# Which engine issues the stores of a DiT block kernel: from one queue to three

## The chip, the cores and the metric

The kernel runs on one core of one Trainium2 chip. The metric is the device time of one execution in microseconds (us); less is better. A core has five engines that run side by side, each through its own instruction stream in order: TensorE (PE, matmuls), VectorE (DVE), ScalarE (ACT), GpSimd (POOL) and SyncE (SP), which here issues DMAs and nothing else. A DMA moves data between HBM and the on-chip memory; it is issued by an instruction on one of these streams, and an instruction that has to wait for its data holds everything behind it in the same stream.

## The reference

One layer of a diffusion backbone, in float32: 2048 latent tokens of width 1024, and 256 context tokens that only supply the initial states of a scan.

```python
hx = modulate(rmsnorm(x, pre_norm_mix), mx[0], mx[1])
# token_mixers:
proj = h @ w_in
xbc = silu(dwconv(proj[..., OFF_XBC:OFF_DT], conv_w, conv_b))
y = y_f + y_b[:, ::-1] + d_skip[:, None] * xs      # a chunked scan in either direction
y = rmsnorm(y * silu(z), ssm_g)
p = pool_mixer(proj[..., OFF_POOL:], w_pool, pool_scale)   # box means on a 32x64 grid, minus the token
yx = concatenate([y, p]) @ w_out
x = x + mx[2] * rmsnorm(yx, post_norm_mix)
hx = modulate(rmsnorm(x, pre_norm_ffn), mx[3], mx[4])
# conv_ffn:
v, g = split(dwconv(hx @ w_up, conv_w, conv_b), 2)
x = x + mx[5] * rmsnorm((silu(g) * v) @ w_down, post_norm_ffn)
```

## The kernel before, in words

**Matmuls.** A float32 product is made of three passes: each operand is split into a high half (ScalarE, L120) and a low half (the rest, L123, on VectorE or GpSimd), and `mm3` (L151 to L153) multiplies high by high, high by low and low by high into the same PSUM bank. A low half is thus needed from the second pass (L152) on.

**Stages.** Times are those of the profiled execution.

- 0 to 560: the input projection in four blocks of 512 tokens, with the convolutions and the forward scan. Block 0 splits the weights (`wunit`, L130 to L139) and stores both halves to `wk_d`; blocks 1 to 3 load them back (L141). `pool_unit` writes `u_d` (L569) and `c_d` (L582); the scan writes `sb_d` (L535) and `y_d` (L544); the gate writes `sz_d` (L795).
- 556 to 680: `pool_mix`, eight steps (four groups, two halves): load a piece of `c_d` into a region of `XB` (L597) and one of `u_d` (L601), add shifted copies (L606), subtract (L615), multiply (L620), scale on ScalarE (L621), store `p_d` (L622). The region of `XB` is used again two steps later, and so L597 waits for the store of L622.
- 600 to 930: the backward scan, the product with `w_out`, the residual (`x1_d`, L837), the norm (`h_d`, L906) and sums of quarters (`hs_d`, L889).
- 975 to 1400: the up projection, upper half (p=1), as one level of a Strassen scheme with seven products per pair; 22 pairs. Four sums of weights per pair are split and kept in `wu_d` (L1072); the result goes to `act_d` (L1122).
- 1400 to 1837: the lower half (p=0), 11 steps of two pairs. The kept weights come back from `wu_d` (L1068). A step stores two tiles of `act_d` (L1124), and `act_sums` stores four sums to `s_d` (L1143); `down_sums` stores `ds_d` (L1152).
- 1837 to 2298: the down projection, again seven products. Its tiles `ar` come from `s_d` and `act_d` (L1203), its weights `rw` from `ds_d` or from the weight itself (L1191); both are split into `as` and `tc`. The rows of the result are stored to `out` (L1226).

**What sets the order.** The code is written as streams of work with priorities (`hot()`, `high_priority`). A scheduler with a simulated time line puts the instructions of each engine into an order before the program runs. On the chip each engine takes its list strictly in that order. Tiles live in small rings (six for `wo`, three for `ar`): an instruction that writes a tile waits until its former readers, a store among them, are done.

**Queues.** All loads and stores are issued by SyncE, about 1020 instructions in one list. A store there waits for the engine that makes its data, and the loads behind it wait with it. GpSimd (`G` in the code) makes small copies in the up stages: the two columns between the halves (L1104, L1105, L1107, L1108), one column of a sum (L1137) and of the last column (L1126). ScalarE is `S`, VectorE `V`.

## Time and profile before

| | us |
|---|---|
| median of 3 runs | 2299.97 (2297.82, 2299.97, 2303.13) |
| the profiled execution | 2301.18 |
| its span in the trace | 2298.1 |
| around the span | 3.1 |
| TensorE busy | 2117.2 (92%) |
| VectorE busy | 1639.7 (71%) |
| ScalarE busy | 902.8 (39%) |
| GpSimd busy | 452.1 (20%) |

A span is the time from the first to the last instruction in the trace. Busy shares are averages over stages that differ: a table by stage shows where TensorE stands still, and the list of its waits says what ended each stand-still. In the table by stage the columns after the busy times are the granted clock of TensorE as a share of full speed (PEclk; 1.00 is 2.4 GHz), the mean busy share of the DMA engines, and what they moved in GB/s. A timeline then gives the single instructions of one engine, with start and duration; the brackets behind a row hold the idle time before it and what ended it. "SPq" is SyncE's queue; a duration there is the time in which one DMA (or x2, two of them) was being issued, waits between the two included.

### The profile page before, as it was taken

Reading aid. Unit: us, or ns where it says so; the run is one execution under the profiler, and the core shown is the slowest. Engines: PE = TensorE matmul, PEld = TensorE weight load, DVE = VectorE, ACT = ScalarE, POOL = GpSimd, SP = SyncE. Lnnn points to the kernel's source line nnn. Section 1 sums busy time; section 2 is a strip of 40 time slices with the busy share of each in tenths; the row PEclk is TensorE's granted clock in tenths of the full one; section 3 lists DMA queues with packets and bytes.
Section 4 is the critical chain, followed back from the end, with each engine's and each line's share of the span. In section 5 each row is a group of like instructions: output and inputs, shape, how many; then the busy total and the mean of one; then the engine's idle time right before and its main releaser. Section 6 shows DMA issues by size and latency. Waiting matters only on the chain. (4 is left out here: it accounts for less than half of the span.)

```text
span 2298.1 us, 27242 instructions
## 1 busy us (share of the span) xinstructions
PE 2117.2 (92%) x9473; PEld 1684.1 (73%) x9473; DVE 1639.7 (71%) x2464; ACT 902.8 (39%) x1372; POOL 452.1 (20%) x553
## 2 busy tenths in 40 slices
PE   8798999899778788499999999999999969999998
PEld 4686777677456666388888887878888758888786
DVE  5777868977778567678878888878767654333666
ACT  4434433333324544445444445323333334333422
POOL 1533524525355443000001001000000000000000
PEclk9989999899899899799999999999999989999999
DMA  8856969869774658765566669999777585444364
GB/s 307 273 181 241 311 226 346 262 218 285 251 233 149 236 191 281 271 217 206 213 247 219 239 224 335 381 348 358 257 262 259 193 292 181 140 151 139 124 231 148
DMA packets 242970, 552.91 MB, mean 241 GB/s; under 512 B 52176, under 2 KB 101008, under 8 KB 238480
## 3 DMA queue, kind: packets, MB, share of 16 engines
q1 hardware_dynamic: 242832, 551.17, 68.2%
q8 instruction: 74, 1.21, 0.2%
q14 instruction: 64, 0.52, 0.1%
HBM read 369.56 MB, written 181.54 MB: 240 GB/s over the span
## 5 line engine op out<-in xcount | busy, mean ns | idle before, releaser
L152 PE MATMUL pu<-xcT,wo 128*128 128x512 f32 x704 | 278.7, 396 | 0.0
L151 PE MATMUL pu<-xcT,wo 128*128 128x512 f32 x704 | 278.6, 396 | 0.0
L153 PE MATMUL pu<-xcT,wo 128*128 128x512 f32 x704 | 276.9, 395 | 0.0
L151 PE MATMUL pu<-xcB,wo 128*128 128x512 f32 x528 | 210.1, 399 | 25.4 <-ACT wo L120 21.1
L151 PE MATMUL psf<-tc,as 128*128 128x512 f32 x528 | 204.5, 395 | 21.7 <-ACT tc L120 21.5
L123 DVE TENSOR_TENSOR as<-ar,as 128x1024 fp32r<-128x1024 f32 x66 | 80.8, 1224 | 193.6 <-ACT as L120 193.5
L152 PE MATMUL pu<-xcB,wo 128*128 128x512 f32 x528 | 210.0, 398 | 0.0
L153 PE MATMUL pu<-xcB,wo 128*128 128x512 f32 x528 | 208.4, 397 | 0.3 <-DVE wo L123 0.3
L152 PE MATMUL psf<-tc,as 128*128 128x512 f32 x528 | 206.0, 390 | 0.0
L151 PE MATMUL pu<-wh,hxh 128*128 128x512 f32 x384 | 156.2, 423 | 29.0 <-DVE eb L817 10.8
L153 PE MATMUL psf<-tc,as 128*128 128x512 f32 x528 | 179.7, 391 | 3.0 <-DVE as L123 3.0
L153 PE MATMUL pu<-hxh,wl 128*128 128x512 f32 (+2 forms) x448 | 165.1, 371 | 2.3 <-POOL wl L123 2.1
L123 POOL TENSOR_TENSOR wl<-wst,wh 128x1024 fp32r<-128x1024 f32 x48 | 122.6, 2554 | 225.9 <-ACT wh L120 202.3
L151 PE MATMUL pu<-hxh,wh 128*128 128x512 f32 (+2 forms) x448 | 164.9, 373 | 2.0 <-ACT wh L120 1.4
L152 PE MATMUL pu<-hxl,wh 128*128 128x512 f32 (+2 forms) x448 | 166.3, 372 | 0.0
L152 PE MATMUL pu<-wl,hxh 128*128 128x512 f32 x384 | 159.4, 415 | 5.3 <-POOL wl L123 5.3
L151 PEld LDWEIGHTS pu<-xcT,wo 128*128 128x128 f32 x704 | 132.9, 189 | 31.3 <-ACT wo L120 0.3
L152 PEld LDWEIGHTS pu<-xcT,wo 128*128 128x128 f32 x704 | 133.0, 189 | 31.1
L153 PEld LDWEIGHTS pu<-xcT,wo 128*128 128x128 f32 x704 | 132.5, 188 | 31.1
L153 PE MATMUL pu<-wh,hxl 128*128 128x512 f32 x384 | 153.9, 409 | 0.0
L120 ACT CAST as<-ar 128x1024 fp32r<-128x1024 f32 x66 | 69.5, 1054 | 214.5 <-PE psf L153 191.0
L120 ACT CAST wo<-rawu 128x512 fp32r<-128x512 f32 x132 | 81.6, 620 | 174.3 <-PE pu L153 168.6
(326 smaller groups left out, 4589.0 us busy)
## 6 DMA issues: line engine op xcount, KB each, us to landing
wu_d<-wo SPq DMA_DIRECT2D x88, 512.0 KB, 2.7
wo<-wu_d SPq DMA_DIRECT2D x88, 512.0 KB, 5.5
rawu<-in_w_up_dram SPq DMA_DIRECT2D x66, 512.0 KB, 4.0
wh<-wk_d SPq DMA_DIRECT2D x48, 512.0 KB, 6.7
wl<-wk_d SPq DMA_DIRECT2D x48, 512.0 KB, 5.8
ar<-s_d SPq DMA_DIRECT2D x44, 512.0 KB, 3.5
XB<-in_w_ada_b_dram SPq DMA_DIRECT2D x32, 512.0 KB, 6.3
wst<-in_w_out_dram SPq DMA_DIRECT2D x32, 512.0 KB, 4.7
```

The costliest lines, as they stand in the source:

```text
L120: S.copy(out=hi, in_=src)
L123: le.tensor_tensor(out=lo, in0=src, in1=hi.bitcast(F32), op=ALU.subtract)
L151: PE.matmul(o, lt[0], rt[0], start=start, stop=False, **kw)
L152: PE.matmul(o, lt[0], rt[1], start=False, stop=False, **kw)
L153: PE.matmul(o, lt[1], rt[0], start=False, stop=stop, **kw)
```

## The change

Every store but five instructions leaves SyncE. Stores of what ScalarE makes, and some others beside it, are issued by ScalarE (`S.dma_start`); the rest is issued by GpSimd (`G.dma_start`). On SyncE stay all loads, the two small stores of `gr_d`, and the last three rows of the output. In number, 108 DMAs go to ScalarE's stream, 104 of them in the first 930 us; about 270 go to GpSimd's. Nothing is computed in another way. The diff, without its lines of context:

```diff
@@ -134,9 +134,9 @@
-                for t, d_ in zip((hi, lo), kept):
+                for t, d_, e in zip((hi, lo), kept, (S, le)):
-                        nc.sync.dma_start(out=d_, in_=t.bitcast(F32))
+                        e.dma_start(out=d_, in_=t.bitcast(F32))
@@ -400,7 +400,7 @@
-            nc.sync.dma_start(out=rows_d, in_=csT)
+            S.dma_start(out=rows_d, in_=csT)
@@ -532,7 +532,7 @@
-            nc.sync.dma_start(out=sb_d[c * P:(c + 1) * P, :], in_=sb)
+            S.dma_start(out=sb_d[c * P:(c + 1) * P, :], in_=sb)
@@ -541,7 +541,7 @@
-            nc.sync.dma_start(out=y_d[c * P:(c + 1) * P, :], in_=y)
+            G.dma_start(out=y_d[c * P:(c + 1) * P, :], in_=y)
@@ -566,7 +566,7 @@
-        nc.sync.dma_start(out=u_d[g * P:(g + 1) * P, b * TB:(b + 1) * TB].rearrange("p (r c) -> p r c", c=GW),
+        S.dma_start(out=u_d[g * P:(g + 1) * P, b * TB:(b + 1) * TB].rearrange("p (r c) -> p r c", c=GW),
@@ -579,7 +579,7 @@
-        nc.sync.dma_start(out=c_d[g * P:(g + 1) * P, b * TB:(b + 1) * TB].rearrange("p (r c) -> p r c", c=GW),
+        G.dma_start(out=c_d[g * P:(g + 1) * P, b * TB:(b + 1) * TB].rearrange("p (r c) -> p r c", c=GW),
@@ -619,7 +619,7 @@
-        nc.sync.dma_start(out=p_d[g * P:(g + 1) * P, cols], in_=d)
+        S.dma_start(out=p_d[g * P:(g + 1) * P, cols], in_=d)
@@ -757,7 +757,7 @@
-                    nc.sync.dma_start(out=ct_d[:, :, b * TB:(b + 1) * TB], in_=CT)
+                    S.dma_start(out=ct_d[:, :, b * TB:(b + 1) * TB], in_=CT)
@@ -792,7 +792,7 @@
-            nc.sync.dma_start(out=sz_d[b * TB + i * P:b * TB + (i + 1) * P, :], in_=o)
+            S.dma_start(out=sz_d[b * TB + i * P:b * TB + (i + 1) * P, :], in_=o)
@@ -834,7 +834,7 @@
-                    nc.sync.dma_start(out=self.dst[t0:t0 + P, cs], in_=self.ys[i][:, cs])
+                    G.dma_start(out=self.dst[t0:t0 + P, cs], in_=self.ys[i][:, cs])
@@ -886,7 +886,7 @@
-        nc.sync.dma_start(out=hs_d[p][:, :, kk, :].rearrange("s p c -> p s c"), in_=hb)
+        G.dma_start(out=hs_d[p][:, :, kk, :].rearrange("s p c -> p s c"), in_=hb)
@@ -903,7 +903,7 @@
-            nc.sync.dma_start(out=h_d[b // 2][k, :, b % 2 * TB:(b % 2 + 1) * TB], in_=full[:, 0:TB])
+            S.dma_start(out=h_d[b // 2][k, :, b % 2 * TB:(b % 2 + 1) * TB], in_=full[:, 0:TB])
@@ -1037,7 +1037,7 @@
-        nc.sync.dma_start(out=h_d[0][:, :, i * P:(i + 1) * P].rearrange("k p t -> p k t"),
+        S.dma_start(out=h_d[0][:, :, i * P:(i + 1) * P].rearrange("k p t -> p k t"),
@@ -1069,7 +1069,7 @@
-                nc.sync.dma_start(out=wu_d[i][a - 1], in_=w.bitcast(F32))
+                G.dma_start(out=wu_d[i][a - 1], in_=w.bitcast(F32))
@@ -1119,9 +1119,9 @@
-            nc.sync.dma_start(out=dst[:, 1:2 * TB], in_=v[:, 0:2 * TB - 1])
+            G.dma_start(out=dst[:, 1:2 * TB], in_=v[:, 0:2 * TB - 1])
-            nc.sync.dma_start(out=dst, in_=v[:, 0:2 * TB])
+            G.dma_start(out=dst, in_=v[:, 0:2 * TB])
@@ -1140,7 +1140,7 @@
-            nc.sync.dma_start(out=s_d[q_][k], in_=o_)
+            G.dma_start(out=s_d[q_][k], in_=o_)
@@ -1149,7 +1149,7 @@
-        nc.sync.dma_start(out=ds_d[k], in_=t)
+        G.dma_start(out=ds_d[k], in_=t)
@@ -1172,7 +1172,7 @@
-    nc.sync.dma_start(out=act_d[1][1][:, :, 0].rearrange("k p -> p k"), in_=last)
+    G.dma_start(out=act_d[1][1][:, :, 0].rearrange("k p -> p k"), in_=last)
@@ -1223,7 +1223,7 @@
-            nc.sync.dma_start(out=out[t0:t0 + P, :], in_=y)
+            (nc.sync if th and j > 4 else G).dma_start(out=out[t0:t0 + P, :], in_=y)

```

**The entry to the down stage.** SyncE's list before, from the last load of kept weights of the up stage to the third tile of the down stage (`act_d_87` to `act_d_90` are the four parts of `act_d`; `s_d_91` to `s_d_94` the four sums; what stands behind a name is its number):

```order
L1068 DMA wo<-wu_d_3_185 128x1024
L1124 DMA act_d_87<-av 128x1024
L1124 DMA act_d_89<-av 128x1024
L1175 DMA act_d_90<-last 128x11x1
L1143 DMA s_d_91<-tt 128x1024
L1143 DMA s_d_93<-tt 128x1024
L1143 DMA s_d_92<-av 128x1024
L1143 DMA s_d_94<-av 128x1024
L1203 DMA ar<-s_d_92 128x1024
L1191 DMA rw<-ds_d 128x512
```

The same place of SyncE's list after the change:

```order
L1136 DMA tt<-act_d_88 128x1023
L1136 DMA tt<-act_d_90 128x1023
L1068 DMA wo<-wu_d_3_185 128x1024
L1203 DMA ar<-s_d_92 128x1024
L1191 DMA rw<-ds_d 128x512
```

The seven stores between the last `wo` and the first `ar` are gone from it. They now stand in GpSimd's list, between its copies:

```order
L1124 DMA act_d_87<-av 128x1024
L1137 COPY tt<-av 128x1
L1124 DMA act_d_89<-av 128x1024
L1126 COPY last<-av 128x1
L1137 COPY tt<-av 128x1
L1175 DMA act_d_90<-last 128x11x1
L1143 DMA s_d_91<-tt 128x1024
L1143 DMA s_d_93<-tt 128x1024
L1143 DMA s_d_92<-av 128x1024
L1143 DMA s_d_94<-av 128x1024
```

The store of `act_d_89` now comes before the two copies, which VectorE's first sum needs. On ScalarE and VectorE the order of this stretch is the same in both kernels.

**The pool mixer.** SyncE's list before, around the second and the third store of the upper groups:

```order
L544 DMA y_d<-y 128x512
L622 DMA p_d<-XB 128x1024
L601 DMA xr<-u_d 128x1024
L141 DMA wl<-wk_d_1_211 128x1024
L130 DMA wst<-in_w_out_dram 128x1024
L597 DMA XB<-c_d 128x1536
L622 DMA p_d<-XB 128x1024
```

ScalarE's list after the change, at this place (`DMAHW` is a counter of landed DMAs, eight of which SyncE and ScalarE share, so that a DMA waits for the one eight before it on its counter; for 55 of ScalarE's 108 DMAs that one is a load of SyncE):

```order
L621 ACTIVATE XB<-pb,pt 128x512 [waits PE_49]
L622 DMA p_d<-XB 128x1024 [waits DMAHW5_49,Activation_49]
L621 ACTIVATE XB<-pb,pt 128x512 [waits DMAHW3_49,PE_49]
L621 ACTIVATE XB<-pb,pt 128x512 [waits PE_49]
L508 ACT_TABLE_LOAD
```

The store follows the activation that makes its data, in the same list, and the activations behind it come after it.

**The upper half of the up stage.** GpSimd's list after the change, one pair (before, L1105 and L1104 took turns there and nothing else):

```order
L1072 DMA wu_d_1_115<-wo 128x1024
L1122 DMA act_d_88<-av 128x1023
L1072 DMA wu_d_0_114<-wo 128x1024
L1105 COPY sv<-un 128x2
L1072 DMA wu_d_2_116<-wo 128x1024
L1104 MEMSET un 128x2
L1105 COPY sv<-un 128x2
L1072 DMA wu_d_3_117<-wo 128x1024
L1104 MEMSET un 128x2
```

Five stores of 512 KB stand between the four small operations of a pair.

## Rows read from the trace of the kernel before

**Rows 1.** Stages: window, us, busy (count) of PE, PEld, DVE, ACT, POOL, then PEclk.
```profile
0.00:930.00 930.00, 819.68 (x3888) 632.46 (x3889) 693.11 (x1194) 365.88 (x611) 377.49 (x344) 0.94 0.73 250
...
975.00:1400.00 425.00, 425.00 (x1849) 344.06 (x1848) 358.06 (x507) 202.94 (x294) 35.56 (x85) 1.00 0.63 228
...
1837.00:1862.50 25.50, 4.03 (x12) 2.89 (x11) 15.52 (x14) 5.85 (x7) 0.31 (x2) 0.60 0.64 219
```

**Rows 2.** Waits of TensorE, whole span: us in total, times, longest.
```profile
PE psf L151 <- ACT tc L120: 21.5, 1, 21.5
PE pu L151 <- ACT wo L120: 21.1, 1, 21.1
...
PE pb L620 <- DVE XB L615: 9.4, 2, 8.0
...
PE pu L151 <- ACT wh L120: 8.7, 6, 2.4
```

**Rows 3.** Timelines of the engines, 1826 to 1863, by time: start, us, engine, line.
```profile
1826.24 19.26 SPq L1124 DMA_DIRECT2D act_d<-av  x2
...
1842.83 1.06 ACT L1117 ACTIVATE ag<-ag 128x1025 f32<-128x1025 f32 x1 [2.68 <-DVE ag L1113]
1843.92 1.23 DVE L1118 TENSOR_TENSOR av<-av,ag 128x1025 f32<-128x1025 f32 x1 [1.12 <-ACT ag L1117]
...
1849.33 1.22 DVE L1142 TENSOR_TENSOR av<-av 128x1024 f32<-128x1024 f32 x1
1849.33 1.58 SPq L1143 DMA_DIRECT2D s_d<-av  x2
1851.00 0.59 SPq L1203 DMA_DIRECT2D ar<-s_d  x1
...
1856.53 1.04 ACT L120 CAST as<-ar 128x1024 fp32r<-128x1024 f32 x1 [12.64 <-DMA ar<-s_d]
...
1858.26 0.62 ACT L120 CAST tc<-rw 128x512 fp32r<-128x512 f32 x1 [0.69 <-DMA rw<-ds_d]
...
1858.93 3.69 PE L151 MATMUL psf<-tc,as 128*128 128x512 f32 x8 [21.47 <-ACT tc L120]
...
1862.46 0.40 PE L152 MATMUL psf<-tc,as 128*128 128x512 f32 x1
```

**Rows 4.** Timelines of the engines, 570 to 612, by time, around the pool mixer.
```profile
579.38 3.52 SPq L544 DMA_DIRECT2D y_d<-y  x1
...
579.69 0.69 ACT L621 ACTIVATE XB<-pb,pt 128x512 f32<-128x512 f32 x1 [1.18 <-PE pb L620]
...
583.00 0.37 SPq L622 DMA_DIRECT2D p_d<-XB  x1
...
588.23 0.32 SPq L597 DMA_DIRECT2D XB<-c_d  x1
...
610.86 2.05 PE L620 MATMUL pb<-XB,junk 128*128 128x512 f32 x2 [8.02 <-DVE XB L615]
```

**Rows 5.** One source line, L906: count, ns min/median/max, first and last start.
```profile
L906 SPq DMA_DIRECT2D h_d<-t x24: 319/320/671, 784.5 to 919.7; - x24
```

**Rows 6.** Waits of SyncE's queue, whole span: us in total, times, longest.
```profile
SPq L139 <- ACT wh L120: 37.3, 12, 9.3
```

**Rows 7.** One of the costliest groups of the page: count, busy us, mean ns, idle before.
```profile
L123 POOL TENSOR_TENSOR wl<-wst,wh 128x1024 fp32r<-128x1024 f32 x48 | 122.6, 2554 | 225.9 <-ACT wh L120 202.3
```

**Rows 8.** GpSimd's groups by line in 975 to 1400, same columns.
```profile
L1105 POOL COPY sv<-un 128x2 f32<-128x2 f32 x43 | 31.3, 729 | 267.7 <-ACT un L1095 149.7 <-DVE un L1099 118.0
```

**Rows 9.** Timeline of VectorE 570 to 586: one form of L615 twice.
```profile
574.54 2.05 DVE L615 SCALAR_TENSOR_TENSOR XB<-XB,xr 128x1024 f32<-128x1024 f32 x1 [0.63 <-POOL XB L612]
...
582.73 1.22 DVE L615 SCALAR_TENSOR_TENSOR XB<-XB,xr 128x1024 f32<-128x1024 f32 x1
```

**Rows 10.** DMA issues on the page: count, KB each, us to landing.
```profile
wu_d<-wo SPq DMA_DIRECT2D x88, 512.0 KB, 2.7
...
act_d<-av SPq DMA_DIRECT2D x22, 512.0 KB, 5.2
```

## The prediction

> **What bounds the kernel now.** I read the table by stage first. In the up stage TensorE is busy without a gap, 425.00 of 425 us in its first half, at a granted clock of 1.00 [rows 1]. Nothing that a store does there can make it faster; it can only make it slower. The gaps lie elsewhere: the first 930 us, with TensorE busy 819.68 us, so 110 us short, and 25.5 us at the entry to the down stage, with 4.03 us of work [rows 1]. The list of TensorE's waits comes next. It has two waits of 21 us, one for `tc` at the entry to the down stage, one for `wo` at the entry to the up stage; the pool mixer stands at 9.4 us, the weights `wh` at 8.7 us [rows 2]. The first of these I follow in the timeline, since SyncE's queue is part of it; behind the second no store stands: the order of SyncE and ScalarE at the entry to the up stage is the same after the change but for the stores, and its chain runs over splits on VectorE. It is costed at nothing.
>
> **The entry to the down stage.** SyncE issues the two stores of `act_d` as one group from 1826.24 to 1845.50, because the second waits for the product on VectorE (L1118, 1843.92 and 1.23 long). The store of the last sum waits until 1850.5 for VectorE's last sum (L1142, from 1849.33). Only then, at 1851.00, comes the load of the first `ar`, although its data was stored long before. ScalarE gets it at 1856.53, `tc` follows at 1858.26, and TensorE begins at 1858.93 and comes to its second pass at 1862.46 [rows 3].
>
> After the change no store stands ahead of this load; it then waits for the end of a product of the up stage, by 1830, and both loads are there long before ScalarE is free. ScalarE is free at 1842.83 + 1.06 = 1843.9 [rows 3], and its list has the same order as before. So `as` ends at 1844.9, `tc` at 1845.6, and the eight matmuls of the first pass begin at 1845.6 instead of 1858.93. But the second pass needs low halves from VectorE, and there the four sums stand first, in both kernels. The copies on GpSimd that the first of them needs now come after the store of `act_d_89`. With x for the issue of a store on GpSimd, the sums begin at 1845.2 + x + 0.4. The fourth overwrites the tile that this store reads, so it waits for the landing; an `act_d` store landed 5.2 us after its issue in the middle [rows 10]. With x = 0.7 this is 1851.1, its end 1852.3, and two splits of 1.2 and 0.7 us (as the sum and the `tc` of this place) bring the second pass to 1854.2. That is 8.3 us earlier than 1862.46. TensorE has idled twice by then; if it goes once more through eight matmuls at 3.69 / 8 = 0.46 us instead of 0.23, 1.9 us are lost again, of which I take 1.3. **−7.0 us**, ends −9.5 (x = 0.3, a landing that isn't felt) and −3 (x = 3, a landing as late as 7 us).
>
> **The pool mixer.** Here a store on ScalarE follows its data at once. In the trace the activation L621 ended at 580.38, but the store went out at 583.00, behind one of `y_d` that held the queue for 3.52 us; the load that waits for its landing went out at 588.23, and TensorE's wait of 8.02 us at 610.86 stands at the end of what that load began [rows 4]. 583.00 − 580.38 = 2.6 us earlier: **−2.6 us**, ends −8 (the whole wait) and +4, since the stores of `c_d`, which the loads read, now come from GpSimd and may land later.
>
> **Loads out of the stores' shadow.** In the first 930 us SyncE waited for data of stores, with loads behind it: 37.3 us in twelve waits for `wh` alone [rows 6]. TensorE felt late weights with 8.7 us [rows 2]. I give a third of that back: **−3 us**, ends 0 and −15, the bound if most waits for weights and some of the chains behind them go.
>
> **ScalarE's new work.** 104 stores in the first 930 us. An issue took 0.32 us in the middle on SyncE [rows 5], so 33 us more on an engine that is busy 365.88 of 930 [rows 1]. No row shows an issue on ScalarE; I take SyncE's. Between none of it on the path and the busy share of 39% (13 us) I take a tenth, as ScalarE is seldom the last to be waited for: **+3.3 us**. The four late stores of `h_d` (L1040) lie in a stage with 202.94 of 425 us of ScalarE busy, and cost nothing as long as TensorE has its `wo`.
>
> **GpSimd's new work.** 68 stores in the first 930 us. No row shows an issue there. The ends are 0.32 us, SyncE's [rows 5], and 2.55 us, a split of 128x1024 by GpSimd [rows 7]: 22 to 173 us, on 377.49 of 930 busy [rows 1]. I take 0.7 us, nearer to the issue, since it is the same instruction: 48 us, of which a fifteenth lies on the path (the splits of `w_out` behind stores of `x1_d`, which wait for VectorE): **+3.3 us**, ends 0 and +25. The Trainium skill's "DMA: Bandwidth & Descriptors", section "SWDGE vs HWDGE vs iDMA", says that GpSimd builds the descriptors of its DMAs in software; no row here shows it.
>
> **The up stage.** 425 / 22 = 19.3 us a pair, five stores a pair on GpSimd, which has 35.56 / 22 = 1.6 us of work in it [rows 1]. At 0.7 us each it is at 5.1 of 19.3. A tile of `wo` is one of six with 19.3 / 7 = 2.8 us between them; a store landed 2.7 us after its issue [rows 10], so some 11 us of delay are covered by the ring. The copies L1105, 0.73 us in the mean [rows 8], come later by a store or two, and the next user of their tile is a pair away. The second half has seven stores in a step of 437 / 11 = 39.7 us. **0 us**; without that cover it is the second rival.
>
> **The sum.** −7.0 − 2.6 − 3 + 3.3 + 3.3 = −6.0 us, on the profiled execution's 2301.2 (span 2298.1 and 3.1 around it). That one is 1.2 us above the median, so I put the change on the median: 2300.0 − 6.0 = **2294 us**.
>
> **The rivals.**
>
> *ScalarE stalls on its own stores.* Of its 108 stores 55 wait, on a counter shared with SyncE, for a load that was issued eight DMAs earlier; if it is late, ScalarE's arithmetic stands still where SyncE's queue stood before. For it: SyncE's loads wait often, and the lists are made by simulated times. Against it: eight DMAs are mostly old. At 0.5 us each it is 27 us of ScalarE; a third on the path is +9: **2303 us**.
>
> *VectorE becomes the bound of the up stage (slower).* VectorE is busy 358.06 of 425 us in the first half [rows 1], 16.3 of 19.3 us a pair; 3.0 us are free for five stores. If an issue on GpSimd holds VectorE for more than 0.6 us, every pair grows. For it: beside work of GpSimd the same operation L615 took 2.05 instead of 1.22 us [rows 9], 0.83 more; at that, 5 × 0.83 − 3.0 = 1.15 us a pair, 22 pairs: +25, **2319 us**. Against it: those were operations with tiles, and an issue moves none. The Trainium skill's "SBUF — State Buffer", section "SBUF: two separate sides", has it the other way round: while VectorE holds the port that they share, GpSimd can't write its descriptors and the DMA waits. By that the stores land later and VectorE loses nothing; the sum would then lean to the −3 end at the entry to the down stage.
>
> *The first 930 us gain more.* If the loads were what the chains waited for, the −3 goes to −15 and the costs of ScalarE and GpSimd hide: **2282 us**. For it: SyncE's list there loses a third of its instructions. Against it: TensorE's waits name few DMAs.
>
> *Nothing is saved.* By the Trainium skill's "DMA: Bandwidth & Descriptors", section "Issuing engines are not separate DMA queues", DMAs of all engines run on the same 16 DMA engines, and only issue time is saved. As a mechanism here: the early loads at 1830 run beside loads and stores of the up stage, or wait for a tile that isn't free before 1850, and the entry stays as it is; with the other terms +1: **2301 us**. Against it: a tile of this size was on hand 5.5 us after its issue [rows 3], and there are 14 us.
>
> **How the numbers follow.** Forecast (2294, own range 2286 to 2302): 0.42. ScalarE stalls: 0.20. VectorE: 0.12. More gain: 0.18. Nothing saved: 0.08. A measurement of this kernel tells about 0.2% from no change, 4.6 us: below 2295.4 is faster, above 2304.6 slower. Forecast gives 0.26 faster, 0.14 same, 0.02 slower; stalls 0.10 same and 0.10 slower; VectorE 0.12 slower; more gain 0.17 faster and 0.01 same; nothing saved 0.02 faster, 0.04 same, 0.02 slower. Sum: 0.45, 0.29, 0.26. The order of all engines in the first 930 us changes widely, which no row prices. The range from 2279 to 2316 leaves out some 0.08 below and 0.10 above.
>
> **What would show it.** TensorE's wait for `tc` at the entry to the down stage should fall from 21.5 us to about 8, with a second stand-still of some 5 us before L152. Waits for L622 before L597 should shrink. In the up stage TensorE should stay at 425 of 425 with VectorE's busy time unchanged; if VectorE's operations grow there, the second rival is at work. ScalarE's idle time ended by its own DMA issues shows the first. I am wrong if the stage up to 930 us moves by more than 10 us, or if an issue on GpSimd costs more than about 3 us.

## The result: slower, and the profile after

| | before | after |
|---|---|---|
| median, us | 2300.62 (2297.82 to 2303.13) | 2321.78 (2313.96 to 2324.01) |
| ratio, 95% interval | | 1.0091 [1.0075, 1.0107] |
| profiled execution, its span | 2301.18, 2298.1 | 2313.96, 2312.2 |

The change costs 21 us where the forecast gave a gain of 6; the time lies above the range. The profiled execution of the changed kernel is the lowest of its four times (the others are 2321.59, 2321.98 and 2324.01), so its trace shows 14 of the 21 us. A later kernel with the same front was profiled in a long execution (e4_front_only below).

Four marks on TensorE cut the span into stages. The first product of the up stage (L151 with `xcB`), its last matmul, the first L152 of the down stage, and the last matmul of the kernel:

| | first of the up stage | its length | to the first L152 of the down stage | from there to the last matmul |
|---|---|---|---|---|
| before | 953.4 | 883.7 | 25.4 | 424.8 |
| after | 974.2 | 883.6 | 16.1 | 427.4 |
| difference | +20.9 | −0.1 | −9.3 | +2.6 |

So the late half of the change did what the prediction said of it (−9.3 + 2.6 = −6.7 us), and the front lost three times as much in this execution. First the late half. These are the stages of the changed kernel, in the columns of [rows 1]: the first half of the up stage, and the entry to the down stage.

```profile
995.00:1420.00 425.00, 425.00 (x1848) 343.87 (x1847) 358.28 (x507) 201.68 (x294) 92.54 (x196) 1.00 0.64 229
1857.90:1873.90 16.00, 4.13 (x11) 2.54 (x9) 13.45 (x13) 5.74 (x7) 4.09 (x8) 0.59 0.48 162
```

TensorE is busy for 425.00 of 425 us as in [rows 1]. GpSimd's busy time has grown from 35.56 to 92.54 us, and VectorE's has stayed where it was, 358.28 against 358.06.

The timelines of the engines at the entry to the down stage, after the change, by time (columns as in [rows 3]):

```profile
1849.99 0.32 SPq L1203 DMA_DIRECT2D ar<-s_d  x1
1850.36 0.42 SPq L1191 DMA_DIRECT2D rw<-ds_d  x1
...
1863.57 1.06 ACT L1117 ACTIVATE ag<-ag 128x1025 f32<-128x1025 f32 x1 [2.68 <-DVE ag L1113]
1864.53 1.03 ACT L120 CAST as<-ar 128x1024 fp32r<-128x1024 f32 x1
1865.47 0.61 ACT L120 CAST tc<-rw 128x512 fp32r<-128x512 f32 x1
1866.13 3.78 PE L151 MATMUL psf<-tc,as 128*128 128x512 f32 x8 [7.93 <-ACT tc L120]
1866.19 0.53 POOL L1124 DMA_DIRECT2D act_d<-av  x1 [17.84 <-DVE av L1118]
...
1870.84 1.22 DVE L1142 TENSOR_TENSOR av<-av 128x1024 f32<-128x1024 f32 x1
1873.85 0.80 PE L152 MATMUL psf<-tc,as 128*128 128x512 f32 x1 [3.94 <-DVE tc L123]
```

Compared with [rows 3]: the load of `ar` goes out 14.6 us before ScalarE is free (L1117 ends at 1863.57 + 1.06 = 1864.63) and not 7.1 us after it. ScalarE splits `as` and `tc` at once, and the wait of 21.47 us falls to 7.93. Then comes a second stand-still of 3.94 us, for the low half behind the four sums. The first L152 and the nine matmuls behind it run slowly again (most 0.43 us apart, 0.23 before; the granted clock is 0.67 in the first 6.1 us from this L152, where it was 1.00); they take 2.0 us more than before, most of the 2.6 us in the last column of the table.

The front is where the time went. The largest waits of TensorE in the changed kernel (columns as in [rows 2]):

```profile
PE pu L151 <- ACT wo L120: 27.2, 1, 27.2
PE pu L151 <- ACT wh L120: 22.1, 5, 7.7
PE pb L620 <- DVE XB L615: 14.0, 1, 14.0
...
PE psf L151 <- ACT tc L120: 7.9, 1, 7.9
```

Against [rows 2], `wh` has grown from 8.7 to 22.1, the pool mixer from 9.4 to 14.0, and the wait at the entry to the up stage from 21.1 to 27.2. At the pool mixer, the timelines of ScalarE's and SyncE's DMAs and TensorE show this:

```profile
597.98 0.67 ACT L621 ACTIVATE XB<-pb,pt 128x512 f32<-128x512 f32 x1
598.68 0.33 ACTq L622 DMA_DIRECT2D p_d<-XB  x1
...
604.42 1.48 SPq L597 DMA_DIRECT2D XB<-c_d  x2
...
628.48 2.04 PE L620 MATMUL pb<-XB,junk 128*128 128x512 f32 x2 [13.99 <-DVE XB L615]
```

The store follows its activation at once, as was predicted. But two loads L597 now stand in a pair in SyncE's list, and TensorE waits 13.99 us where it waited 8.02 [rows 4].

And the issues themselves: GpSimd's groups by line in 975 to 1420, columns as in [rows 8]; a DMA issue of the page, columns as in [rows 10]; and a source line with ScalarE's stores (of e2_before_order, an experiment below; columns as in [rows 5]).

```profile
L1072 POOL DMA_DIRECT2D wu_d<-wo x88 | 47.0, 534 | 127.0 <-DVE wo L123 123.3 <-issue 2.2 <-DVE un L1093 0.3
L1122 POOL DMA_DIRECT2D act_d<-av x21 | 11.4, 545 | 40.7 <-DVE av L1118 40.5 <-DVE wo L123 0.3
```

```profile
wu_d<-wo POOLq DMA_DIRECT2D x88, 512.0 KB, 3.5
```

```profile
L906 ACTq DMA_DIRECT2D h_d<-t x24: 326/326/359, 801.6 to 941.6; - x24
```

An issue took 0.53 us on GpSimd in the up stage (0.7 was taken) and 0.326 us on ScalarE (0.32 was taken).

### The profile page after: what moved, and what is told of

Read it like the earlier page. It is cut to its first block, busy times and chain, and to the rows that moved or that the text cites. A ratio compares the mean times of both kernels' runs of the same rounds, so it can differ in the third digit from the quotient of the medians.

```text
span 2312.2 us, 27271 instructions
## 1 busy us (share of the span) xinstructions
PE 2123.6 (92%) x9473; PEld 1687.5 (73%) x9473; DVE 1645.1 (71%) x2464; ACT 897.7 (39%) x1369; POOL 588.1 (25%) x826
## 3 DMA queue, kind: packets, MB, share of 16 engines
q0 software_dynamic: 36784, 144.19, 16.1%
## 5 line engine op out<-in xcount | busy, mean ns | idle before, releaser
L151 PE MATMUL pu<-xcT,wo 128*128 128x512 f32 x704 | 278.9, 397 | 0.0
L152 PE MATMUL pu<-xcT,wo 128*128 128x512 f32 x704 | 278.8, 396 | 0.0
L153 PE MATMUL pu<-xcT,wo 128*128 128x512 f32 x704 | 277.3, 395 | 0.0
L151 PE MATMUL pu<-xcB,wo 128*128 128x512 f32 x528 | 210.5, 399 | 32.7 <-ACT wo L120 27.2
L151 PE MATMUL psf<-tc,as 128*128 128x512 f32 x528 | 204.0, 394 | 8.5 <-ACT tc L120 7.9
L152 PE MATMUL psf<-tc,as 128*128 128x512 f32 x528 | 206.8, 392 | 3.9 <-DVE tc L123 3.9
L152 PE MATMUL pu<-xcB,wo 128*128 128x512 f32 x528 | 209.7, 397 | 0.0
L153 PE MATMUL pu<-xcB,wo 128*128 128x512 f32 x528 | 207.5, 396 | 1.2 <-DVE wo L123 1.2
L153 PE MATMUL psf<-tc,as 128*128 128x512 f32 x528 | 180.3, 395 | 3.0 <-DVE as L123 3.0
L151 PE MATMUL pu<-wh,hxh 128*128 128x512 f32 x384 | 156.6, 422 | 22.4 <-ACT wh L120 19.1
L153 PE MATMUL pu<-hxh,wl 128*128 128x512 f32 (+2 forms) x448 | 167.8, 376 | 4.3 <-POOL wl L123 4.3
L151 PE MATMUL pu<-hxh,wh 128*128 128x512 f32 (+2 forms) x448 | 166.0, 376 | 4.0 <-ACT wh L120 3.0
L152 PE MATMUL pu<-hxl,wh 128*128 128x512 f32 (+2 forms) x448 | 167.6, 375 | 0.0
L152 PE MATMUL pu<-wl,hxh 128*128 128x512 f32 x384 | 159.8, 416 | 7.8 <-POOL wl L123 7.8
L153 PE MATMUL pu<-wh,hxl 128*128 128x512 f32 x384 | 155.8, 414 | 2.1 <-DVE hxl L123 2.1
L151 PEld LDWEIGHTS pu<-xcT,wo 128*128 128x128 f32 x704 | 132.9, 189 | 31.6 <-ACT wo L120 0.3
L152 PEld LDWEIGHTS pu<-xcT,wo 128*128 128x128 f32 x704 | 132.9, 189 | 31.1
L153 PEld LDWEIGHTS pu<-xcT,wo 128*128 128x128 f32 x704 | 132.6, 188 | 31.1
```

The lines of the kernel that those rows point to most:

```text
L151: PE.matmul(o, lt[0], rt[0], start=start, stop=False, **kw)
L152: PE.matmul(o, lt[0], rt[1], start=False, stop=False, **kw)
L153: PE.matmul(o, lt[1], rt[0], start=False, stop=stop, **kw)
```

## The experiments

Several theories for the front remained: (1) the issues on GpSimd lie on the path; (2) those on ScalarE do; (3) the scheduler's other order costs, and the stores nothing; (4) single stores land later from their new queue and hold whoever waits for them. To separate stores from order, some kernels fix the order. They build a first program with all stores on SyncE, take each engine's list from it, and chain every instruction but the moved stores to its forerunner in that list:

```diff
-    V, S, G, PE = nc.vector, nc.scalar, nc.gpsimd, nc.tensor
+    V, S, G, PE = nc.vector, nc.scalar, nc.gpsimd, nc.tensor; SQ, GQ = (S, G) if MOVED else (nc.sync, nc.sync)
...
+def _pin(tc, nc, order):
+    """Every engine's instructions, moved stores aside, go out in the order given."""
+    at = {i.name: i for i in nc.cur_bb.bb.instructions}
+    last = {}
+    for name in order:
+        i = at.get(name)
+        if i is None:
+            continue
+        if i.engine in last:
+            tc.add_manual_dep(i, last[i.engine].name, mybir.DependencyInfo(
+                mybir.DependencyClass.NoSync, mybir.DependencyReason.DATA), reason="order")
+        last[i.engine] = i
```

A moved store is issued by `SQ` or `GQ`; the scheduler still finds its place between the fixed instructions. Below, "fixed" means this. That the fixing costs nothing by itself is seen in e7_late_pinned, where no store of the front moves: its up stage begins at 953.0 us, and at 953.4 before. All ratios are to the kernel before on the same chip; us are ratio less 1, times 2300. A ratio is estimated from all executions and can differ from that of the two medians (most for e3_after_order, whose medians are 9.7 us apart and whose ratio gives 11.7).

**e1_late_only.** Only the stores of the up and the down stage move (L1040 to L1226), the scheduler orders freely. One of the edits:

```diff
-            nc.sync.dma_start(out=dst, in_=v[:, 0:2 * TB])
+            G.dma_start(out=dst, in_=v[:, 0:2 * TB])
```

> Only the stores of the up and down stages move (L1040 to ScalarE; L1072, L1122, L1124, L1143, L1152, L1175, L1226 to GpSimd); the first 930 us keep SyncE and the order of before. Theory A (the loss of 21 us lies in the first 975 us, the entry to the down stage gained 7.4 us): about 7 us faster than before, 2293 us, 954 us until the first product of the up stage, as before. Theory B (stores on GpSimd cost something in the up and down stages too, hidden in the profiled run): 2300 us or more.

Measured: 2298.29 against 2299.29, 0.9997 [0.9985, 1.0009]. The entry to the down stage is as short as in the changed kernel (16.0 us), but the up stage takes 889.4 us where it took 883.7. Its lower half is ordered otherwise: in 1400 to 1640 TensorE was busy 232.73 us, 235.70 before. Its waits for L1087 in the up stage grew from 4.3 to 5.5 us, and two on VectorE, of 0.9 and 0.8 us, are new; VectorE's own busy time in this stretch is 191.57 us in both. The time lies between the two theories: the gain was there and was given back, and e7_late_pinned shows that the order gave it back.

**e2_before_order.** All stores move as in the changed kernel, all else is fixed in the order of before. One of the edits:

```diff
-        nc.sync.dma_start(out=c_d[g * P:(g + 1) * P, b * TB:(b + 1) * TB].rearrange("p (r c) -> p r c", c=GW),
+        GQ.dma_start(out=c_d[g * P:(g + 1) * P, b * TB:(b + 1) * TB].rearrange("p (r c) -> p r c", c=GW),
```

> Stores on the engines of the changed kernel, but every other instruction of each engine, loads included, in the order of before. Theory A1 (the scheduler's new order of the first 930 us is what costs 21 us and more): the loss goes, the gain stays: 2293 to 2298 us, first product of the up stage by 960 us. Theory A2 (issues on ScalarE and GpSimd, their waits and late landings cost it): the loss stays: 2315 to 2325 us.

Measured: 2316.62 against 2299.29, 1.0077 [1.0059, 1.0095], +18 us. The old order doesn't save the front: the up stage begins at 978.4. So the moved stores alone are enough for a loss, as Theory A2 said.

**e3_after_order.** The reverse: all stores stay on SyncE, all else is fixed in the order of the changed kernel.

```diff
-    first, _, was = _program(False, arrs)
-    _, _, now = _program(True, arrs)
+    first, _, was = _program(True, arrs)
+    _, _, now = _program(False, arrs)
```

> All stores on SyncE as before, but every other instruction in the order of the changed kernel; the scheduler places the stores among SyncE's loads. Theory A1: the loss is there without any store moved: 2315 to 2330 us, first product of the up stage at 970 us or later. Theory A2: 2296 to 2303 us.

Measured: 2309.02 against 2299.29, 1.0051 [1.0033, 1.0068], +12 us. The order made for moved stores costs too, where the stores are not moved. The time lies between the ranges of the two theories: each is right in part. Its list of waits of TensorE shows which of the waits above belong to the order:

```profile
PE pu L151 <- ACT wo L120: 25.8, 1, 25.8
...
PE pu L151 <- ACT wh L120: 16.6, 5, 6.2
...
PE pb L620 <- DVE XB L615: 14.1, 1, 14.1
```

These are the waits of the changed kernel, in a kernel in which no store has moved. With the order of before they are back near [rows 2] when ScalarE's stores move (e5_act_front: 20.8 for `wo`, 9.8 for `wh`, 9.4 for the pool mixer) or GpSimd's (e6_pool_front: 23.2, 10.4, 9.0); when both do, the first two in part and the pool mixer's hardly at all (e2_before_order: 23.7, 12.9, 13.5).

**e4_front_only.** The complement of e1: the stores up to L906 move, the late ones stay, free order. One of the edits:

```diff
-            nc.sync.dma_start(out=h_d[b // 2][k, :, b % 2 * TB:(b % 2 + 1) * TB], in_=full[:, 0:TB])
+            S.dma_start(out=h_d[b // 2][k, :, b % 2 * TB:(b % 2 + 1) * TB], in_=full[:, 0:TB])
```

> Only the stores of the first 930 us move (L139 to L906); those of the up and down stages stay on SyncE. Both theories: the loss without the gain, the changed kernel's 2322 us and 7 more, 2329 us, first product of the up stage at 974 us. If it is 2320 or less, part of the loss came from the later stages.

Measured: 2324.89 against 2299.29, 1.0118 [1.0094, 1.0142], +27 us, 4 us less than was expected. The entry to the down stage is at its old 25.5 us. Its profiled execution, the highest of its four, begins the up stage at 987.4; the changed kernel, with the same front, at 974.2. Single executions scatter by up to some 10 us (here 2322.79 to 2331.65, the kernel before on the same chip 2295.14 to 2304.83), so a mark in one profile is good to that, and the medians decide.

**e5_act_front and e6_pool_front.** Order of before; of the front's stores only the 104 of ScalarE move, or only the 68 of GpSimd:

```diff
-    V, S, G, PE = nc.vector, nc.scalar, nc.gpsimd, nc.tensor
+    V, S, G, PE = nc.vector, nc.scalar, nc.gpsimd, nc.tensor; SQ, GQ = (S, nc.sync) if MOVED else (nc.sync, nc.sync)
```

```diff
-    V, S, G, PE = nc.vector, nc.scalar, nc.gpsimd, nc.tensor
+    V, S, G, PE = nc.vector, nc.scalar, nc.gpsimd, nc.tensor; SQ, GQ = (nc.sync, G) if MOVED else (nc.sync, nc.sync)
```

> Order of before on every engine; of the first 930 us' stores only ScalarE's 104 move, GpSimd's 68 stay on SyncE, and so do all later stores. In the run with both moved at the order of before, the first product of the up stage came 23 to 25 us later than with neither. Theory S (ScalarE's issues, 0.33 us each, and waits in its stream cost it): 12 to 23 us later here, 2312 to 2322 us. Theory G (GpSimd's issues, 0.53 to 0.94 us each, and the heads of its queue cost it): up to 6 us later, 2299 to 2305 us.

> Order of before on every engine; of the first 930 us' stores only GpSimd's 68 move. Theory S: up to 6 us later at the first product of the up stage, 2299 to 2305 us. Theory G: 12 to 23 us later, 2312 to 2322 us. If the two runs together come to the 23 us, the costs add; if less, one hides the other or they meet.

Measured: ScalarE's stores 2310.57 against 2298.75, 1.0052 [1.0038, 1.0066], +12 us; GpSimd's 2316.91, 1.0073 [1.0058, 1.0089], +17 us. Both cost, each more than its 3.3; the first lies between the two theories, the second where Theory G put it. Together they come to 28.8 us, against 17.7 + 6.2 = 23.9 when both move at once (e2_before_order, less the late gain of e7_late_pinned); the intervals are too wide to tell whether one hides part of the other. Of e6_pool_front, GpSimd's groups in 0 to 980 that are DMAs (busy us, mean ns, idle before them and what ended it):

```profile
L582 POOL DMA_DIRECT2D c_d<-upad x16 | 15.1, 945 | 3.7 <-POOL upad L580 2.1 <-issue 1.1 <-POOL upad L567 0.2
L544 POOL DMA_DIRECT2D y_d<-y x16 | 9.6, 603 | 20.0 <-DVE y L543 15.5 <-DVE gd L523 2.2 <-DVE r L166 2.2
L139 POOL DMA_DIRECT2D wk_d<-wl x16 | 9.5, 593 | 3.2 <-POOL wl L123 2.1 <-POOL raw L318 0.7 <-POOL raw L310 0.3
...
L837 POOL DMA_DIRECT2D x_d<-eb x8 | 4.7, 583 | 9.4 <-DVE eb L835 9.4
L837 POOL DMA_DIRECT2D x_d<-XB x8 | 4.5, 568 | 26.8 <-DVE XB L835 26.8
L889 POOL DMA_DIRECT2D hs_d<-XB x4 | 3.1, 772 | 5.1 <-DVE XB L888 3.8 <-DMA wst<-in_w_out_dram 1.3
```

The busy times sum to 46.5 us, near the 48 of the prediction; +17 us is a share of 0.36. In front of the stores of `y_d` and `x1_d` (the groups `y_d` and `x_d`) GpSimd stands idle for another 56 us until VectorE has made the data. What stands behind them in its list waits too; whether it was ready wasn't followed.

**e7_late_pinned.** As e1, but with all else fixed in the order of before.

```diff
-                G.dma_start(out=wu_d[i][a - 1], in_=w.bitcast(F32))
+                GQ.dma_start(out=wu_d[i][a - 1], in_=w.bitcast(F32))
```

(from e1_late_only to e7_late_pinned, here and at the other late stores; and `_pin`.)

> Only the stores of the up and down stages move, and every other instruction keeps the order of before, in the up stage too, where the run without that gave back 5.7 us. Theory: the entry to the down stage gains 7.4 us and nothing else changes: 2291 to 2294 us, up stage 882 to 884 us long. Rival: the stores on GpSimd cost the up stage what the other run lost there, whatever the order: 2298 us, up stage 889 us.

Measured: 2293.01 against 2298.75, 0.9973 [0.9964, 0.9982], −6.2 us, as its theory said. This version beats both kernels. Its timeline of TensorE at the entry to the down stage:

```profile
1843.02 3.78 PE L151 MATMUL psf<-tc,as 128*128 128x512 f32 x8 [7.93 <-ACT tc L120]
1850.75 0.79 PE L152 MATMUL psf<-tc,as 128*128 128x512 f32 x1 [3.95 <-DVE tc L123]
```

The same two stand-stills as in the changed kernel; the up stage begins at 953.0 and takes 881.7 us.

**e8_act_no_ud and e9_ud_only.** Order of before; ScalarE's 88 stores of the front without the 16 of `u_d`, and those 16 alone:

```diff
-        nc.sync.dma_start(out=u_d[g * P:(g + 1) * P, b * TB:(b + 1) * TB].rearrange("p (r c) -> p r c", c=GW),
+        SQ.dma_start(out=u_d[g * P:(g + 1) * P, b * TB:(b + 1) * TB].rearrange("p (r c) -> p r c", c=GW),
```

(this edit alone is e9_ud_only; all others of ScalarE without it are e8_act_no_ud.)

> As the run with ScalarE's 104 front stores moved at the order of before (11.8 us slower), but u_d (L569, rows of 256 bytes, sixteen stores) stays on SyncE. In that run u_d landed as late as 16.6 us after its issue (9.6 before), and GpSimd's waits for it went from 29 to 53 us. Theory U (the late landing of u_d, in a queue of its own beside SyncE's, is the cost): within 3 us of before, 2297 to 2302 us. Theory S (the 0.33 us that each issue holds ScalarE): 88 of 104 issues are still there, so 2307 to 2311 us.

> Order of before; the sixteen stores of u_d alone on ScalarE. Theory U: 6 to 12 us slower than before, 2305 to 2311 us, GpSimd's waits for u_d at 45 us or more. Theory S: sixteen of 104 issues, 1 to 2 us, 2299 to 2301 us.

Measured against 2301.12: the 88 stores 2304.79, 1.0013 [1.0004, 1.0023], +3 us; the 16 of `u_d` 2306.80, 1.0028 [1.0017, 1.0039], +6.4 us, though they are 6 us of issues. The second is where Theory U put it, the first between the two theories. The source line L569 (count, ns, first and last start, and the landings) and the waits of GpSimd for it. Before:

```profile
DMA to landing us min/median/max: 2.6/6.8/9.6
```

```profile
POOL upad L574 <- DMA u_d<-upad: 30.6, 7, 15.4
```

With `u_d` on ScalarE (e9_ud_only):

```profile
L569 ACTq DMA_DIRECT2D u_d<-upad x16: 366/366/448, 67.1 to 563.1; - x16
...
DMA to landing us min/median/max: 2.6/8.8/14.0
```

```profile
POOL upad L574 <- DMA u_d<-upad: 50.4, 8, 20.0
```

One of these, before and then in e9_ud_only (timelines of ScalarE, the issuing queue and GpSimd):

```profile
229.40 0.58 ACT L568 COPY upad<-pu 128x512 f32<-128x512 f32 x1
...
231.59 0.82 SPq L569 DMA_DIRECT2D u_d<-upad  x1
...
239.14 3.83 POOL L574 TENSOR_TENSOR upad<-upad 128x624 f32<-128x624 f32 x3 [15.41 <-DMA u_d<-upad]
```

```profile
230.55 0.58 ACT L568 COPY upad<-pu 128x512 f32<-128x512 f32 x1
...
231.16 0.37 ACTq L569 DMA_DIRECT2D u_d<-upad  x1
...
245.14 4.41 POOL L574 TENSOR_TENSOR upad<-upad 128x624 f32<-128x624 f32 x3 [20.04 <-DMA u_d<-upad]
```

L574 overwrites the tile that the store reads. Before, it starts 7.6 us after the issue; from ScalarE's queue the store leaves 1.6 us sooner after its copy, and L574 starts 14.0 us after it. GpSimd stands still until then, and its later work in this stretch, the scan and the low halves among it, is queued behind L574. The sizes speak for this wait as what makes most of the 6.4 us (a tenth of 6 us of issues is 0.6, and GpSimd's waits for the landing grew by 19.8), but no kernel takes it away alone.

**e10_pool_no_cd and e11_cd_only.** The same cut through GpSimd's stores: 52 without `c_d`, and the 16 of `c_d` alone (L582, the edit shown at e2).

> As the run with GpSimd's 68 front stores moved at the order of before (18 us slower), but c_d (L582, sixteen stores, 0.94 us an issue) stays on SyncE. Theory G (time that GpSimd's stream loses: 44 us with c_d, 29 without): two thirds of the loss stay, 2309 to 2313 us. Theory C (c_d alone, by its long issue and its landing): 2298 to 2304 us.

> Order of before; the sixteen stores of c_d alone on GpSimd. Theory G: a third of the loss of 18 us, 2304 to 2307 us. Theory C: 2311 to 2317 us.

Measured against 2301.12: 2311.45, 1.0046 [1.003, 1.0061], +10.6 us for 31 us of issues, where Theory G put it; and 2308.48, 1.0032 [1.0018, 1.0047], +7.4 us for 15 us, 1 us above Theory G's range. The cost is a third to a half of the issue time, and no single store makes it. GpSimd makes the data of `c_d` itself, so it hardly stands in front of these stores (its group in e11_cd_only, columns as above):

```profile
L582 POOL DMA_DIRECT2D c_d<-upad x16 | 15.0, 939 | 3.4 <-POOL upad L580 3.3
```

**e12_ud_gpsimd.** The 16 stores of `u_d` alone, from GpSimd instead of ScalarE:

```diff
-        nc.sync.dma_start(out=u_d[g * P:(g + 1) * P, b * TB:(b + 1) * TB].rearrange("p (r c) -> p r c", c=GW),
+        GQ.dma_start(out=u_d[g * P:(g + 1) * P, b * TB:(b + 1) * TB].rearrange("p (r c) -> p r c", c=GW),
```

> Order of before; the sixteen stores of u_d alone, on GpSimd instead of ScalarE (where they landed 8.8 us after the issue in the middle and 14.0 at most, against 6.8 and 9.6 from SyncE, and GpSimd waited 50 us for them, against 31). Theory Q (rows of 256 bytes land late from any queue but the loads' own): landing 8 us or more, GpSimd's waits 45 us or more, 2306 to 2312 us. Theory R (only ScalarE's queue delays them): landing near 7 us, waits near 30 us; what is left is sixteen issues of 0.94 us on GpSimd, as for c_d alone, 2304 to 2309 us.

Measured: 2308.29 against 2299.96, 1.0038 [1.002, 1.0056], +8.7 us. GpSimd's group of these stores, their landings and its wait for them:

```profile
L569 POOL DMA_DIRECT2D u_d<-upad x16 | 14.9, 930 | 31.6 <-ACT upad L568 29.1 <-ACT sb L478 2.5
```

```profile
DMA to landing us min/median/max: 3.4/7.2/8.8
```

```profile
POOL upad L574 <- DMA u_d<-upad: 20.6, 7, 6.4
```

From GpSimd the stores land about as before, and L574 waits 10 us less than before, which is Theory R; yet the kernel is as slow as with `u_d` on ScalarE. In place of the wait GpSimd now has 14.9 us of issues, and it stands idle for 31.6 us in front of them, most of it until ScalarE has made the data (L568). Here the late landing goes with ScalarE's queue, not with having left SyncE's.

| what moved (order) | us | interval |
|---|---|---|
| late stores (free) | −0.7 | −3.5 to +2.1 |
| late stores (before) | −6.2 | −8.3 to −4.1 |
| front, all (free) | +27.1 | +21.6 to +32.7 |
| front, ScalarE's 104 (before) | +12.0 | +8.7 to +15.2 |
| of these, 88 without `u_d` | +3.0 | +0.9 to +5.3 |
| of these, `u_d` | +6.4 | +3.9 to +9.0 |
| front, GpSimd's 68 (before) | +16.8 | +13.3 to +20.5 |
| of these, 52 without `c_d` | +10.6 | +6.9 to +14.0 |
| of these, `c_d` | +7.4 | +4.1 to +10.8 |
| `u_d` alone, on GpSimd (before) | +8.7 | +4.6 to +12.9 |
| nothing (after) | +11.7 | +7.6 to +15.6 |
| all (before) | +17.7 | +13.6 to +21.9 |
| all (free: the change) | +20.9 | +17.3 to +24.6 |

## Why the prediction was wrong, step by step

**The entry to the down stage was right** (−7.0 predicted). The second pass comes 9.3 us earlier and 2.6 us are lost behind it, −6.7 in the changed kernel's profile; alone, with the order kept, e7_late_pinned measures −6.2. The chain was also as described: a wait of 7.9 us (about 8), then one of 3.9 (some 5), then slow matmuls once more (1.9 predicted at most, 1.3 taken, 2.0 measured). One step of it didn't happen: the fourth sum was to wait for the landing of the store of `act_d`, but the four sums ran without a gap (the last at 1870.84, 4.7 us after that store's issue at 1866.19). So the second pass came 9.3 us earlier and not 8.3, which about balances the 2.6 lost behind it, where 1.3 was taken.

**The up stage was right** (0) in this order: 883.6 against 883.7 us, TensorE at 425.00 of 425; in the free order of e1_late_only it took 889.4. The second rival, VectorE as the bound, is refuted where it was to show: VectorE's busy time grew by 0.22 us in 425 beside five stores a pair on GpSimd. The Trainium skill's "SBUF — State Buffer", section "SBUF: two separate sides", says of DMAs issued by GpSimd that GpSimd can't write their descriptors while VectorE holds the port that they share; that VectorE loses nothing here agrees with it, and that stores land 3.5 us after the issue instead of 2.7 (`wu_d`) doesn't speak against it.

**GpSimd's new work is the term that failed most.** The count and the issues were right (68 stores, 46.5 us measured, 48 predicted). The share on the path was not: a fifteenth was taken, 3.3 us; e6_pool_front measures 16.8, a share of 0.36, within the end of +25 that the prediction gave. For ScalarE the prediction had named the busy share of the engine as a bound. For GpSimd that is 377.49 / 930 = 41% [rows 1], which would have given 48 × 0.41 = 20 us; that this comes near is luck, as the same rule gives ScalarE's 88 stores 11 us, and they cost 3.0. The engine was treated as one that nobody waits for because TensorE's list of waits names it with little. But the forward scan, the convolutions' edges and the low halves go through it, and most of its delays arrive at TensorE under another engine's name: in e6_pool_front no wait of TensorE has grown by more than 3.5 us, and the one for GpSimd's `wl` at L152 went from 5.3 to 6.4. Up to the first product of the up stage, the table by stage shows of before

```profile
0.00:953.40 953.40, 822.02 (x3898) 633.99 (x3898) 711.27 (x1223) 376.46 (x626) 377.49 (x344) 0.93 0.74 251
```

and of e6_pool_front

```profile
0.00:971.80 971.80, 831.08 (x3897) 637.74 (x3897) 729.68 (x1223) 376.78 (x626) 415.27 (x414) 0.92 0.72 247
```

The stretch is 18.4 us longer. Half of it, 9.1 us, is TensorE busy longer with the same matmuls, at a granted clock of 0.92 instead of 0.93 (as behind the stand-stills at the entry to the down stage; where in the front they lie wasn't followed), and only the other half is idle time, in many small pieces. A list of waits sorted by size doesn't show such a cost.

That GpSimd's stores cost 16.8 us is shown; by which path they reach TensorE stays open. Three things come with these stores and aren't separated: the issues, GpSimd's standing in front of a store whose data another engine hasn't made, and VectorE, whose busy time grew in every kernel in which GpSimd issues stores of the front (by 18.4 us here, 4.6 in e10_pool_no_cd, 5.9 in e11_cd_only, 8.9 in e12_ud_gpsimd; by 1.5 in e5_act_front, where only ScalarE does). The second isn't needed for a cost: in e11_cd_only GpSimd stands idle for 3.4 us in front of the stores, and they cost 7.4 for 15.0 us of issues. Nor does it add in proportion: 31.6 us of it in e12_ud_gpsimd come with 8.7.

**ScalarE's new work was right but for one store.** A tenth of 88 issues is 88 × 0.33 × 0.1 = 2.9 us, and e8_act_no_ud measures 3.0 [0.9, 5.3]; the interval takes in shares from 0.03 to 0.18. What was missed is `u_d`: +6.4 us, since it lands later from ScalarE's queue (at most 14.0 us after its issue, 9.6 before) and GpSimd's L574 waits for the landing. The prediction looked for ScalarE's own stalls (the first rival: stores that wait on the counter shared with SyncE); from the end of what ScalarE did before to the start of its 108 stores, 8.2 us pass in all in the changed kernel, 2.8 at most, where the rival had 27. So that mechanism is refuted; that all 104 cost 12.0, about the rival's 3.3 + 9, is chance. For the stores of `act_d`, `p_d`, `c_d` and `wu_d` the prediction asked who waits for the landing, for `u_d` it didn't.

**The pool mixer (−2.6) and the loads out of the shadow (−3) gave nothing, in either order.** The store of `p_d` did go out with its activation. But the load that it was to release waits for its landing. In e8_act_no_ud, at the order of before, the place of [rows 4] looks like this (ScalarE and SyncE):

```profile
580.45 0.69 ACT L621 ACTIVATE XB<-pb,pt 128x512 f32<-128x512 f32 x1 [1.12 <-PE pb L620]
...
581.17 0.33 ACTq L622 DMA_DIRECT2D p_d<-XB  x1
...
588.43 0.32 SPq L597 DMA_DIRECT2D XB<-c_d  x1
```

The store starts as its activation ends, and the load goes out 7.3 us after that, where it was 7.9 before: of the 2.6 us 0.6 are left, since the landing came 7.2 us after the issue instead of 5.2, and TensorE's wait is 8.5 instead of 8.0. SyncE's waits of L597 for `p_d`, which were to shrink, went from 14.4 us to 25.6 in the changed kernel and 16.1 in e2_before_order. With the loads of weights it is another wait that takes the place of the stores. SyncE's waits in the first 990 us, of before and then of e2_before_order, all stores moved:

```profile
SPq L141 <- PE pu L153: 65.1, 21, 9.2
```

```profile
SPq L141 <- PE pu L153: 140.0, 33, 14.7
```

The loads come to their turn sooner, and then wait until TensorE's last pass (L153) is done with the tile that they fill. TensorE's wait for `wh`, 8.7 us before, is 8.6 to 26.1 in the kernels with moved stores of the front. In the changed kernel both waits of TensorE even grew, to 14.0 and 22.1. e3_after_order has 14.1 and 16.6 with every store on SyncE, and with the old order e2_before_order has 13.5 and 12.9: for `wh` the scheduler's new order accounts for most of the growth, for the pool mixer the order alone is enough, and so are the moved stores of both engines together. That order was called a thing "which no row prices", and the sum took it at nothing. Alone it costs 11.7 us. What it adds on top of the moved stores is less: the front of e4_front_only costs 27.1, that of e2_before_order 23.9 if its late half gains as e7_late_pinned does, and so 3 us, within the intervals. The terms overlap, and the order's part in the changed kernel is somewhere between 3 and 12 us.

**The entry to the up stage was costed at nothing**, and its wait grew by 6.1 us. e3_after_order has 25.8 of the 27.2, so the order alone is enough for most of this; with the order of before and moved stores it is 20.8 to 23.7.

**The sum with measured terms**: −6.2 (late stores, order kept) + 27.1 (front) = +20.9 us, and the change itself measures +20.9. That the two agree so closely is chance, as each term is good to a few us; the −6.2 is taken, and not the −0.7 of the free order, because the up stage of the changed kernel lost nothing (883.6 us). The third rival (more gain in the first 930 us) and the fourth (nothing saved at the entry) are refuted, the one by the sign, the other by 21.5 to 7.9 us. (The third rival's 2282 us has the −15 only; with the costs of ScalarE and GpSimd hidden as well, its terms give 2300.0 − 7.0 − 2.6 − 15 = 2275.) The prediction's own test, a front that moves by more than 10 us, struck: it moved by 20.9 in one profile and 34.0 in another.

## What to carry to other kernels

Move a store out of a queue of loads where the trace shows a load standing behind it that the critical engine waits for; here that was one place, and moving the stores of that stage alone, with all else kept in order, is the version that gains (0.9973). Ask what else such a load waits for: in the front it was the tile that it fills, and taking the stores away gave nothing. A store issued by a compute engine costs issue time on that engine, and neither the bound engine's list of waits nor the engine's busy share tells how much of it reaches the end. GpSimd and ScalarE were both busy for some 40% of the front; of GpSimd's issue time 0.34 to 0.58 reached the end in four kernels, of ScalarE's 0.1 (`u_d` aside). Ask, too, who waits for the landing of a moved store (`u_d`). Where a scheduler makes the order, price the new order by itself: fix the old one and move the stores, and fix the new one and leave them.

## What the runs showed of the hardware

- An issue took 0.326 us on ScalarE's stream and 0.53 to 0.60 on GpSimd's for most stores; for stores in rows of 256 bytes it took 0.37 on ScalarE's (`u_d`) and 0.93 to 0.95 on GpSimd's (`u_d`, `c_d`).
- The same 16 stores of `u_d` landed 2.6/6.8/9.6 us (least, middle, most) after the issue from SyncE, 2.6/8.8/14.0 from ScalarE and 3.4/7.2/8.8 from GpSimd. For `p_d` the difference was small: 3.5/5.3/7.3 from SyncE, 2.7/5.0/7.5 from ScalarE (e8_act_no_ud). Why `u_d` is late, stays open; the page of the changed kernel shows ScalarE's DMAs as a queue of their own (q10), of short packets (packets, MB, share; in the mean 1.07 KB beside 2.45 KB in SyncE's q1):

```profile
q1 hardware_dynamic: 151232, 371.19, 46.7%
...
q10 hardware_dynamic: 33600, 35.79, 4.4%
```

- In the up stage VectorE lost nothing beside 92.54 us of GpSimd, mostly issues. In the front its busy time up to the first product of the up stage was higher where GpSimd issued stores (729.68 us in e6_pool_front, 711.27 before; with the stores of ScalarE alone 712.73): the arithmetic of L326 on 128x512 took 911 ns in the mean instead of 859. The issues alone don't do that: in e6_pool_front seven of these 128 ran beside an issue of GpSimd and none of its arithmetic, and took 749 ns in the mean, against 747 for the 65 with GpSimd idle. The 45 beside its arithmetic alone took 1052, and the eleven beside arithmetic and an issue 1410, one of them 4.95 us. So the longer ones are among those beside GpSimd's arithmetic.
